# Two transformer layers on one core: where the mixer's fillers stop, and how the compressed queries leave PSUM

## The chip, the cores and the metric

The kernel runs on one core of a Trainium2 chip. All times are device microseconds (us) of one execution. Three timed runs of the kernel before gave 1578.85 us as their median (1576.09 to 1584.00). The execution that was profiled took 1582.09 us; its span, from the first to the last instruction, is 1580.3 us.

Engines are named as in the profile: PE is the matrix engine (PEld its weight loads), DVE the vector engine, ACT the scalar engine, POOL and SP two more whose queues mostly issue DMAs here.

## The reference

Two layers of a diffusion trunk over 512 latent and 128 context tokens, width 1024, all in fp32. One layer is

```
h   = rms_norm(x) * (1 + scale) + shift        # modulation = silu(c) @ w_ada + b_ada
p   = h @ w_in                                 # one projection, split into three head groups
A   = windowed attention, 8 heads, sink         # queries q, keys k, values v
B   = real part of a 2-D Fourier transform      # 256 columns f
C   = latent attention (MLA), 4 heads:
        cq, ckv = rms_norm(compressed q), rms_norm(compressed kv)
        q = cq @ w_uq  (64 plain + 32 rotary columns a head);  k, v = ckv @ w_ukv
x   = x + gate * (concat(A, B, C) @ w_o)
x   = x + gate * mlp(rms_norm(x) * (1 + scale) + shift)   # gated, with a width-3 convolution
```

## The kernel before, in words

**Three passes for each product.** Every fp32 matrix product is three fp32r matmuls: each operand is split into a high part (a rounding copy on ACT) and a low part (source minus high part, on DVE). `hilo` issues that pair: one ACT copy at L125, one DVE subtraction at L144. For weights the same split writes `wh` (ACT) and `wl` (DVE, L188).

**The order of the work.** Each layer has a mixer (attention groups A, B and C; in the span about 80 to 320 us for layer 0 and 870 to 1070 us for layer 1), then the output projection and the MLP, which are dense matmuls. In the mixer a pipeline runs ten units of group A and then five of group C. Each is a chain of scores (PE), maximum (DVE), exponential (ACT), normalisation, transposes (PE, L1051 for A and L1126 for C; copied out as `PT`) and products with the values (PE, L983). While a unit waits for its softmax, other PE work is put in by a generator, `filler()`: the query projections, `fourier`, the compressed projections `cqA`, `cqB` and `ckv`, `rest`, the first part of the output projection (`po0` to `po3`, `part1`), `kv` and `k1` (`mla_kv`) and, in layer 0 only, the modulation chunks 4 to 9 (`ada_pe`). The string `CFG[l]["order"]` gives their sequence.

How much filler goes into a place is decided by `pulls(gen, us)` (L262): it adds up the costs that the generator yields until they reach `us`. A yield of `0` lets the pull go on; a yield of `1e9` ends it. Two places (`pre_c0`, `pre_h2`) pull in a loop with `next(fa)` and ignore the costs. The instructions are then scheduled for each engine by priority, so the final order on an engine is read from the built program.

**What the change touches.**
- `ada_pe` (L307 on): a modulation chunk is 8 matmuls with `wa` tiles loaded by SP (L301, 256 KB each), L320, in four column groups that run side by side, an ACT copy `adasb`, then four transposes (L330).
- `fourier` (L893 on): two products into PSUM, their splits `Z`, then a product with `Z` (`mm<-Z,dftc`).
- `rest` (L795 on): sums of squares by tiny matmuls (L801 to L803), two square roots on ACT (L806, L807), reciprocal and a diagonal on DVE, a spread over PE (L383), the normalised compressed kv (`CL`, `CX`), then three groups `m` of compressed queries, 12 matmuls each (`mm<-cqh,wh` and so on). Group 2 is the rotary part: copied out as `qr`, rotated by four DVE instructions (L639 to L642), split from SBUF. Groups 0 and 1 are the plain part of two heads each.

**Buffers.** `MM()` hands out accumulators for large products from a pool of two; `PS()` small PSUM tiles `s` from a pool of four. `CQ[h]` is the split query of head h. A `part1` accumulator is released by `resid` (L537 on DVE, three instructions for 640 columns).

Of the kernel before, what the change touches and what calls it, by code (L numbers as in the profile page):

```python
# [21 lines left out]
HF = 320  # L22
# [56 lines left out]
def hybrid_step(ctx: ExitStack, tc: tile.TileContext, I, O):  # L79
# [10 lines left out]
    def S(name, dt=F32, w=NT):  # L90
        return sp.tile([128, w], dt, tag="S", name=name)
# [26 lines left out]
    def halves(ap):  # L118
        return ap.rearrange("p (a b) -> p a b", a=2)
# [4 lines left out]
    def acopy(out, in_):  # L124
        return nc.scalar.activation(out, in_, AF.Copy)  # L125
# [10 lines left out]
    def pin(i, on=True):  # L136

        if on:
            tc.keep_in_program_order(i)
        return i  # L140

    def hilo(hi, lo, src, fix=False):
        pin(acopy(hi, src), fix)
        nc.vector.tensor_sub(lo, src, f32(hi))  # L144
# [55 lines left out]
    for l in range(L):  # L200
# [6 lines left out]
        for n in CFG[l]["order"].split():  # L207
# [6 lines left out]
            elif n[:2] == "po":  # L214
                i = int(n[2])
# [88 lines left out]
    def ada_pe(l, chunks, ahead=4):  # L304
        todo = [(n, k) for n in chunks for k in range(8)]
        got = {}

        def load(m):
            while todo and len(got) < m:
                e = todo.pop(0)  # L310
                got[e] = ada_load(l, *e)

        load(ahead)
        yield 0.0
        for n in chunks:
            ps = PS()
            for k in range(8):
                j = k % 4
                t = got.pop((n, k))
                pin(nc.tensor.matmul(ps[32 * j:32 * j + 32, :], lhsT=sT[:, k, :], rhs=t, start=(k < 4), stop=(k >= 4)), l == 0 and n < 4)  # L320
                load(ahead)
                if k % 2:
                    yield 0.45
            lead = l == 0 and n < 4
            sb = S("adasb", w=512)
            pin(acopy(sb, ps), lead)
            yield 0.0
            pt = PS()
            for a in range(4):
                pin(nc.tensor.transpose(pt[:, a * 128:(a + 1) * 128], sb[:, a * 128:(a + 1) * 128], ident), lead)  # L330
            pv = pt.rearrange("p (a j v) -> p a v j", a=4, j=4, v=32)[:, :, 0:2, :]
            parts = ((8 + 2 * n, 0, 2), (2 * n, 2, 2)) if lead else ((4 * n, 0, 4),)
            for i, a, w in parts:
                pin(nc.vector.reduce_sum(out=mod[l][:, i:i + w], in_=pv[:, a:a + w], axis=AX.X), lead)
            for i, a, w in parts:
                m = mod[l][:, i:i + w]
                pin(nc.vector.tensor_add(m, m, P(l, "bada")[:, i:i + w].unsqueeze(2).to_broadcast([128, w, 2])), lead)
                if lead:
                    mod_fin(l, i // 8, (i % 8, w))
            if not lead:  # L340
                mod_fin(l, n // 2, (4 * (n % 2), 4))
            yield -1.0
# [332 lines left out]
    def mixer(l, norm, begun, xsrc):  # L675
# [63 lines left out]
        m = MM()  # L739
# [8 lines left out]
        for t in range(5):  # L748
# [4 lines left out]
            f = S("F", F32R, 512)  # L753
# [12 lines left out]
        CQ, CK, CKX, CV = {}, {}, {}, {}  # L766
# [29 lines left out]
        def rest():  # L796
            ckv = st["ckv"]
            ps = PS()
            for b in range(5):
                sl = slice(QCOL[b], QCOL[b] + 128)  # L800
                nc.tensor.matmul(ps[:, 2 * b:2 * b + 2], lhsT=sq["k"][:, sl], rhs=ones[:, 0:2], start=True, stop=True)  # L801
                nc.tensor.matmul(ps[:, 10 + 2 * b:12 + 2 * b], lhsT=sq["A"][:, sl], rhs=ones[:, 0:2], start=True, stop=False)
                nc.tensor.matmul(ps[:, 10 + 2 * b:12 + 2 * b], lhsT=sq["B"][:64, sl], rhs=ones[:64, 0:2], start=False, stop=True)  # L803
            yield 6.0
            rc = SM("rcC", 20, 1)
            nc.scalar.activation(rc[:, :10], ps[:, :10], AF.Sqrt, bias=eps[:, 0:1], scale=1.0 / 128)  # L806
            nc.scalar.activation(rc[:, 10:], ps[:, 10:20], AF.Sqrt, bias=eps[:, 0:1], scale=1.0 / 192)  # L807
            nc.vector.reciprocal(rc, rc)
            st["rq"], st["nrq"] = SM("rq", 10, 1), SM("nrq", 10, 1)
            nc.vector.tensor_scalar_mul(st["rq"], rc[:, 10:], SC_C)  # L810
            nc.vector.tensor_scalar_mul(st["nrq"], rc[:, 10:], -SC_C)
            rf = MM().rearrange("p a b -> p (a b)")
            for b in range(5):
                spread(rf[:, 128 * b:128 * b + 128], rc[:, 2 * b:2 * b + 1])
            yield 2.2
            for c0, c1, r0 in ((0, NL, 0), (CX, NT, NL)):
                nc.vector.scalar_tensor_tensor(out=ckv[:, c0:c1], in0=ckv[:, c0:c1], scalar=P(l, "gckv"), in1=rf[:, r0:r0 + c1 - c0], op0=ALU.mult, op1=ALU.mult)
            nc.gpsimd.dma_start(out=O["sckv"][l], in_=ckv[:, CX:])
            CL = (S("CL", F32R, 512), S("CL", F32R, 512))
            hilo(CL[0], CL[1], ckv[:, :NL])  # L820
            cx = S("CX", F32R, 512)
            CXh, CXl = cx[:, 0:256], cx[:, 256:512]
            hilo(CXh[:, 128:], CXl[:, 128:], ckv[:, CX:])
            t = S("cc", w=NC)
            gated(nc.gpsimd.dma_start(out=t, in_=I["cckv"][l]))
            hilo(CXh[:, :128], CXl[:, :128], t)
            cq = [st["A"], st["B"]]
            wq = W.get(u["uq"])
            for h in range(4):
                CQ[h] = (S("CQ", F32R), S("CQ", F32R))  # L830
            for m in (2, 0, 1):
                ps = MM()
                for hf in range(2):
                    sl = slice(hf * HF, (hf + 1) * HF)
                    for i, (hi, lo, rows) in enumerate(cq):
                        mm3(ps[:, hf, :HF], [w[:rows, i, m * 128:(m + 1) * 128] for w in wq], [hi[:rows, sl], lo[:rows, sl]], i == 0, i == 1)
                    yield 0.82
                if m == 2:
                    f = S("qr")
                    acopy(halves(f), ps[:, :, :HF])  # L840
                    rope(f, 0, 128, "ropeC", swC)
                    for h in range(4):
                        hilo(CQ[h][0][64:96], CQ[h][1][64:96], f[32 * h:32 * h + 32])
                else:
                    for i in range(2):
                        hi, lo = CQ[2 * m + i]
                        hilo(halves(hi[0:64]), halves(lo[0:64]), ps[64 * i:64 * i + 64, :, :HF])
                yield 0.0
            st["kv"] = lambda: mla_kv(CL, CXh, CXl)

# [48 lines left out]
        def fourier(tabs, tx, tch):  # L899
# [12 lines left out]
            for m in range(2):  # L912
                ps = pz[m]
# [3 lines left out]
                    hilo(Z[q][0][:, :258], Z[q][1][:, :258], ps[:, q, :258])  # L917
                    hilo(Z[q][0][:, 258:], Z[q][1][:, 258:], px[:, m * 256 + q * 128:m * 256 + (q + 1) * 128])
                pz[m] = Z
            yield 0  # L920
            for m in range(2):
                Z = pz[m]
                ps = MM()
# [299 lines left out]
        for c in range(8):  # L1223
            ps = Acc()
# [8 lines left out]
    if True:  # L1233
# [22 lines left out]
        for l in range(L):  # L1256
# [81 lines left out]
            for kind, a in u["plan"]:  # L1338
                if kind == "up":
                    for q, cb in (("a", cb_a(a)), ("g", cb_g(a))):  # L1340
                        ps = Acc()
# [12 lines left out]
                if not last:  # L1354
                    for c in range(8):
                        ps = Acc()
# [3 lines left out]
                else:  # L1360
# [7 lines left out]
                    ps = Acc()  # L1368
# [144 lines left out]
```

## Time and profile before

| | |
|---|---|
| median of 3 runs | 1578.85 us (1576.09 to 1584.00) |
| profiled execution | 1582.09 us |
| its span | 1580.3 us |
| PE busy | 1525.2 us, 97% |
| DVE busy | 1116.7 us, 71% |
| ACT busy | 712.3 us, 45% |
| granted PE clock, mean | 0.984 |

PE is nearly always busy, so what can be saved is the time in which it stands still or runs at the lower clock. Both lie almost wholly in the two mixers. A PE row's `[idle before <-releaser]` tells for how long the engine stood still before that row and which instruction ended the wait. Matmul durations overlap, so the cost of one is read from the distance between two starts.

### The profile page before, as it was taken

The page shows a single profiled execution, that of the slowest core. Times are in us where ns is not written, and L with a number is a line of the kernel's source. Part 1 is how long each engine was busy: PE and PEld are TensorE (multiplying, and loading weights), DVE is VectorE, ACT ScalarE, POOL GpSimd, SP SyncE. Part 2 cuts the span into 40 slices and gives each one's busy share as a digit, 9 for nine tenths or more (in the row PEclk, how much of TensorE's full clock was granted, in tenths as well). Part 3 has the DMA queues.
Part 4 walks back from the last instruction along what each step waited for, and adds up shares of the span by engine and source line. Part 5 has one row for each costly group of instructions (what it writes and reads, how often), then busy time and mean ns, then how long its engine had stood idle before and what let it go on. Part 6 is the DMA issues. An engine that isn't in the chain of part 4 may idle for free. (4 is left out here: it accounts for less than half of the span.)

```text
span 1580.3 us, 25827 instructions
## 1 busy us (share of the span) xinstructions
PE 1525.2 (97%) x10082; PEld 1426.3 (90%) x10082; DVE 1116.7 (71%) x2257; ACT 712.3 (45%) x1403; POOL 103.7 (7%) x225
## 2 busy tenths in 40 slices
PE   9999989899999999999999999989999999999997
PEld 7977775599999999999999887869999999999997
DVE  5765674477897888889778777867885466466366
ACT  4555664564432432441445666646433243244142
POOL 1200111100000000001011000120000000000000
PEclk9999999899999999999999999999999999999998
DMA  9542239113334335235244202331332222221211
GB/s 363 166 145 74 73 98 312 56 54 120 116 124 169 120 104 196 104 104 193 81 142 133 72 25 86 114 142 54 120 99 75 81 74 61 94 77 52 100 54 67
DMA packets 61800, 177.59 MB, mean 112 GB/s; under 512 B 7360, under 2 KB 9856, under 8 KB 61680
## 3 DMA queue, kind: packets, MB, share of 16 engines
q1 hardware_dynamic: 44112, 116.41, 22.1%
q0 software_dynamic: 17568, 59.55, 11.2%
q8 instruction: 79, 1.29, 0.3%
q14 instruction: 41, 0.34, 0.1%
HBM read 165.02 MB, written 10.91 MB: 111 GB/s over the span
## 5 line engine op out<-in xcount | busy, mean ns | idle before, releaser
L278 PE MATMUL mm<-hh,wh 128*128 128x320 f32 x1632 | 377.5, 312 | 12.3 <-ACT u L125 9.1
L278 PE MATMUL mm<-hl,wh 128*128 128x320 f32 x1632 | 377.2, 310 | 0.7 <-DVE hl L486 0.4
L278 PE MATMUL mm<-hh,wl 128*128 128x320 f32 x1632 | 376.9, 310 | 0.0
L125 ACT ACTIVATE wh<-wr 128x1024 fp32r<-128x1024 f32 (+2 forms) x189 | 185.9, 984 | 343.1 <-PE mm L278 263.9
L278 PEld LDWEIGHTS mm<-hh,wh 128*128 128x128 f32 x1632 | 273.8, 188 | 20.6 <-ACT u L125 11.0
L278 PEld LDWEIGHTS mm<-hl,wh 128*128 128x128 f32 x1632 | 275.6, 188 | 4.0 <-issue 2.1
L278 PEld LDWEIGHTS mm<-hh,wl 128*128 128x128 f32 x1632 | 274.5, 188 | 3.3 <-issue 3.3
L188 DVE TENSOR_TENSOR wl<-wr,wh 128x1024 fp32r<-128x1024 f32 (+2 forms) x187 | 210.9, 1128 | 48.2 <-ACT wh L125 47.3
L1292 DVE SCALAR_TENSOR_TENSOR y<-u,pk,y 128x642 f32<-128x642 f32 x176 | 156.2, 887 | 67.9 <-ACT y L1289 64.2
L278 PE MATMUL mm<-th,wh 128*128 128x320 f32 x656 | 152.4, 310 | 0.0
L278 PE MATMUL mm<-th,wl 128*128 128x320 f32 x656 | 152.2, 309 | 0.0
L278 PE MATMUL mm<-tl,wh 128*128 128x320 f32 x656 | 152.0, 309 | 0.0
L537 DVE SCALAR_TENSOR_TENSOR x<-mm,mod,x 128x192 f32<-128x192 f32 (+2 forms) x222 | 84.9, 435 | 70.6 <-PE mm L278 70.6
L364 DVE CUSTOM_DVE_ANT_0 junk<-wa,sbc 128x1024 bf16<-128x1024 f32 x112 | 132.1, 1223 | 1.8 <-DMA wa<-in_wat 1.8
L1289 ACT ACTIVATE y<-u,bb,pk 128x513 f32<-128x513 f32 (+1 forms) x176 | 105.9, 650 | 60.8 <-DVE bb L1286 60.8
L278 PEld LDWEIGHTS mm<-th,wh 128*128 128x128 f32 x656 | 110.3, 188 | 0.7 <-ACT th L125 0.4
L278 PEld LDWEIGHTS mm<-th,wl 128*128 128x128 f32 x656 | 110.4, 188 | 0.0
L278 PEld LDWEIGHTS mm<-tl,wh 128*128 128x128 f32 x656 | 110.4, 188 | 0.0
L1282 DVE TENSOR_TENSOR u<-mm,r 128x512 f32<-128x512 f32 (+1 forms) x176 | 79.6, 486 | 42.2 <-PE mm L278 40.1
L125 ACT ACTIVATE u<-mm 128x2 f32<-128x2 f32 x176 | 20.8, 170 | 112.5 <-DVE u L1282 107.5
L1306 ACT ACTIVATE y<-y 128x642 f32<-128x642 f32 x44 | 32.6, 741 | 73.7 <-DVE y L1292 73.7
L361 POOL DMA_DIRECT2D wa<-in_wat x56 | 29.5, 528 | 524.2 <-DVE mod L364 517.8
(311 smaller groups left out, 2195.6 us busy)
## 6 DMA issues: line engine op xcount, KB each, us to landing
wr<-in_wug SPq DMA_DIRECT2D x88, 512.0 KB, 3.5
wa<-in_wat POOLq DMA_DIRECT2D x56, 512.0 KB, 3.8
wa<-in_wa SPq DMA_DIRECT2D x80, 256.0 KB, 5.7
wr<-in_wdn SPq DMA_DIRECT2D x48, 384.0 KB, 3.1
wr<-in_wi SPq DMA_DIRECT2D x16, 512.0 KB, 3.7
wr<-in_wo SPq DMA_DIRECT2D x14, 512.0 KB, 3.7
xpart<-xp POOLq DMA_DIRECT2D x16, 320.0 KB, 3.7
x<-xpart POOLq DMA_DIRECT2D x16, 320.0 KB, 6.1
```

The source lines that it names most:

```text
L125: return nc.scalar.activation(out, in_, AF.Copy)
L188: pin(self.eng.tensor_sub(lo, r, f32(hi)), fix)
L278: pin(nc.tensor.matmul(ps.h[hf][:, :c1 - c0], lhsT=w[wi][:, off[k] if isinstance(off, dict) else k + off, :], rhs=hs[hi][k][:, c0:c1], sta ...
L361: nc.gpsimd.dma_start(out=t, in_=I["wat"][i0 + i])
L364: nc.vector.tensor_tensor_reduce(out=junk, in0=t, in1=sb[v], scale=1.0, scalar=0.0, op0=ALU.mult, op1=ALU.add, accum_out=mod[l][:, n, v:v ...
L537: nc.vector.scalar_tensor_tensor(out=xc[:, c0:c1], in0=ps.h[hf][:, o:o + c1 - c0], scalar=mod[l][:, gidx * 8 + c, v:v + 1], in1=xc[:, c0:c ...
L1282: nc.vector.tensor_mul(halves(uu[:, p:p + n]), ps.t[:, :, o:o + n // 2], halves(nrm.r[:, c0:c1]))
L1289: nc.scalar.activation(y[:, c0:c1], uu[:, c0 + 1:c1 + 1], AF.Identity, bias=bb[:, v:v + 1], scale=cv[:, t, 1:2])
L1292: nc.vector.scalar_tensor_tensor(out=yy, in0=uu[:, q:q + TW], scalar=cv[:, t, q:q + 1], in1=yy, op0=ALU.mult, op1=ALU.add)
L1306: nc.scalar.activation(y, y, AF.Silu)
```

## The change

```diff
@@ ada_pe
             lead = l == 0 and n < 4
             sb = S("adasb", w=512)
             pin(acopy(sb, ps), lead)
-            yield 0.0
+            yield 0.0 if lead else 1e9
             pt = PS()
@@ rest
-            for m in (2, 0, 1):
+            for m in (0, 1, 2):
                 ps = MM()
...
                 else:
+                    f = S("qn")
+                    acopy(halves(f), ps[:, :, :HF])
                     for i in range(2):
-                        hi, lo = CQ[2 * m + i]
-                        hilo(halves(hi[0:64]), halves(lo[0:64]), ps[64 * i:64 * i + 64, :, :HF])
+                        hilo(CQ[2 * m + i][0][0:64], CQ[2 * m + i][1][0:64], f[64 * i:64 * i + 64])
                 yield 0.0
@@ fourier
                 pz[m] = Z
-            yield 0
+            yield 1e9
             for m in range(2):
```

A filler now ends its pull after the copy of a modulation chunk (not for the four leading chunks) and after the splits `Z` of the Fourier product. Groups 0 and 1 of the compressed queries come before the rotary group, and each leaves its accumulator by one ACT copy into an SBUF tile `qn`, from which both splits are then taken (before: two ACT copies and two DVE subtractions straight from PSUM). The number of instructions on PE and DVE is unchanged; ACT has four copies more and two `ACT_TABLE_LOAD` more. Lines below L845 move down by one.

On DVE in layer 0, where the compressed queries are split; before (`CQ<-mm` reads the accumulators `mm_2109` and `mm_2126`, `CQ<-qr` the rotated tile):

```order
L642 TENSOR_TENSOR qr_2094<-qr_2094,ropes_2096 128x512
L144 TENSOR_TENSOR CQ_2058<-mm_2109,CQ_2057 64x640
L144 TENSOR_TENSOR CQ_2058<-qr_2094,CQ_2057 32x640
L188 TENSOR_TENSOR wl_2382<-wr_2183,wh_2381 128x1024
L144 TENSOR_TENSOR CQ_2060<-qr_2094,CQ_2059 32x640
L144 TENSOR_TENSOR CQ_2060<-mm_2109,CQ_2059 64x640
L144 TENSOR_TENSOR CQ_2062<-qr_2094,CQ_2061 32x640
L144 TENSOR_TENSOR CQ_2062<-mm_2126,CQ_2061 64x640
L144 TENSOR_TENSOR CQ_2064<-qr_2094,CQ_2063 32x640
```

And after, the end of the same work on DVE, with the `L537` instructions that release the first `po1` accumulator (`mm_2182`):

```order
L144 TENSOR_TENSOR CQ_2080<-qn_2146,CQ_2079 64x640
L639 STREAM_SHUFFLE ropes_2167<-qr_2165 128x512
L640 TENSOR_TENSOR ropes_2167<-ropes_2167,ropeC_1414 128x512
L641 TENSOR_TENSOR qr_2165<-qr_2165,ropeC_1413 128x512
L144 TENSOR_TENSOR ml_1823<-s_2233,mh_1822 128x128
L642 TENSOR_TENSOR qr_2165<-qr_2165,ropes_2167 128x512
L1037 TENSOR_TENSOR den_2113<-den_2113,d_2115 128x4
L537 SCALAR_TENSOR_TENSOR xp_2180<-mm_2182,mod0_86,xp_2180 128x320
L537 SCALAR_TENSOR_TENSOR xp_2180<-mm_2182,mod0_86,xp_2180 128x192
L144 TENSOR_TENSOR CQ_2074<-qr_2165,CQ_2073 32x640
L144 TENSOR_TENSOR CQ_2076<-qr_2165,CQ_2075 32x640
L144 TENSOR_TENSOR CQ_2078<-qr_2165,CQ_2077 32x640
```

No subtraction reads an accumulator of the compressed queries any more; the rotation and the splits `CQ<-qr` have moved to the end, and a fourth split and the third `L537` follow the rows shown.

On PE at the end of layer 0's fillers, before (`L320` are matmuls of the last modulation chunk, `L330` its transposes, `CKb,CQ` and `CKX,CQ` scores of group C):

```order
L320 MATMUL s<-wa,sT 32x512
L983 MATMUL s<-PT,CV 64x256 x3
L320 MATMUL s<-wa,sT 32x512
L286 MATMUL mm<-CKb,CQ 128x320 x5
L330 MATMUL s<-ident,adasb 128x128 x4
L983 MATMUL s<-PT,CV 64x256 x2
L286 MATMUL mm<-CKb,CQ 128x320
L1126 MATMUL s<-ident,P 128x128 x12
L286 MATMUL mm<-CKb,CQ 128x320 x17
L983 MATMUL s<-PT,CV 64x256 x2
L1126 MATMUL s<-ident,P 128x128 x4
```

And after (the first `L330` is chunk 8's, the second chunk 9's):

```order
L330 MATMUL s<-ident,adasb 128x128 x4
L1127 MATMUL s<-ident,P 128x128 x4
L320 MATMUL s<-wa,sT 32x512 x2
L984 MATMUL s<-PT,CV 64x256 x4
L320 MATMUL s<-wa,sT 32x512 x2
L286 MATMUL s<-CKX,CQ 128x256 x6
L320 MATMUL s<-wa,sT 32x512 x2
L1127 MATMUL s<-ident,P 128x128 x4
L320 MATMUL s<-wa,sT 32x512 x2
L1127 MATMUL s<-ident,P 128x128 x4
L286 MATMUL s<-CKX,CQ 128x256 x3
L330 MATMUL s<-ident,adasb 128x128 x4
```

Chunk 9 has moved into the last softmax units: of the 37 scores `CKb,CQ` that followed it before, 12 still do, and the first scores `CKX,CQ` stand among its matmuls.

On ACT in layer 1, the two square roots of `rest`, before:

```order
L806 ACT_TABLE_LOAD
L806 ACTIVATE rcC<-s,eps 128x10
L807 ACTIVATE rcC<-s,eps 128x10
L1033 ACT_TABLE_LOAD
L1033 ACTIVATE d<-d 128x4
L125 ACTIVATE PT<-s 128x512
```

And after:

```order
L806 ACT_TABLE_LOAD
L806 ACTIVATE rcC<-s,eps 128x10
L1033 ACT_TABLE_LOAD
L1033 ACTIVATE P,den<-s,negm 128x128 x4
L125 ACTIVATE mh<-s 128x128
L807 ACT_TABLE_LOAD
L807 ACTIVATE rcC<-s,eps 128x10
L125 ACTIVATE mh<-s 128x128
```

Four exponentials and two table loads now stand between the two roots. On SP the only difference is in layer 0: where the last 12 loads of `wa` (for chunks 8 and 9) stood in a row ahead of all loads of `wug`, the first `wug` load now stands ahead of the last 12, and the second ahead of the last 10. On POOL loads and stores of `xp` change places in layer 0.

## Rows read from the trace of the kernel before

**Rows 1.** Page, busy time by engine: us, share of the span, instructions.

```profile
PE 1525.2 (97%) x10082; PEld 1426.3 (90%) x10082; DVE 1116.7 (71%) x2257; ACT 712.3 (45%) x1403; POOL 103.7 (7%) x225
```

**Rows 2.** Windows: length, busy time of each engine, granted PE clock, DMA share, GB/s.

```profile
80.00:320.00 240.00, 224.11 (x1364) 169.15 (x1363) 139.82 (x375) 136.42 (x312) 23.50 (x60) 0.95 0.37 124
870.00:1070.00 200.00, 189.19 (x1243) 161.22 (x1243) 148.84 (x380) 121.34 (x282) 23.35 (x60) 0.97 0.26 86
241.00:249.00 8.00, 6.47 (x32) 1.61 (x31) 1.82 (x7) 1.75 (x5) 0.54 (x1) 1.00 1.04 395
278.00:304.00 26.00, 20.44 (x124) 13.62 (x122) 12.15 (x34) 13.59 (x34) 4.90 (x20) 0.92 0.12 44
```

**Rows 3.** Timeline of PE, compressed queries of layer 0: start, duration, instruction, idle before.

```profile
188.25 0.39 PE L286 MATMUL mm<-cqh,wh 128*128 128x320 f32 x1
...
196.46 0.51 PE L1008 MATMUL s<-KH,Q 128*128 128x512 f32 x1
...
202.25 0.87 PE L278 MATMUL mm<-mh,wh 128*128 128x320 f32 x2 [3.67 <-DVE CQ L144]
...
207.72 0.39 PE L278 MATMUL mm<-ml,wh 128*128 128x320 f32 x1
...
210.74 0.45 PE L278 MATMUL mm<-ml,wh 128*128 128x320 f32 x2
211.03 0.46 PE L278 MATMUL mm<-mh,wl 128*128 128x320 f32 x2
```

**Rows 4.** Timeline of DVE at the same place.

```profile
199.18 1.22 DVE L188 TENSOR_TENSOR wl<-wr,wh 128x1024 fp32r<-128x1024 f32 x1
...
201.28 0.82 DVE L144 TENSOR_TENSOR CQ<-mm,CQ 64x640 fp32r<-64x640 f32 x1
...
204.68 0.69 DVE L1011 CUSTOM_DVE_ANT_0 P<-s,mask 128x512 f32<-128x512 f32 x1
...
210.52 1.13 DVE L537 SCALAR_TENSOR_TENSOR xp<-mm,mod,xp 128x320 f32<-128x320 f32 x3
```

**Rows 5.** Timeline of ACT at the same place.

```profile
190.88 0.70 ACT L125 ACTIVATE qr<-mm 128x640 f32<-128x640 f32 x1
```

**Rows 6.** Timeline of PE, Fourier product of layer 0.

```profile
103.29 1.86 PE L286 MATMUL mm<-Z,dftc 128*128 128x386 f32 x7 [1.12 <-DVE Z L144]
```

**Rows 7.** Timeline of PE, modulation chunks 6 and 7.

```profile
241.12 1.07 PE L320 MATMUL s<-wa,sT 128*32 128x512 f32 x8
242.98 0.66 PE L330 MATMUL s<-ident,adasb 128*128 128x128 f32 x4 [0.80 <-ACT adasb L125]
243.56 4.50 PE L320 MATMUL s<-wa,sT 128*32 128x512 f32 x16
248.80 0.66 PE L330 MATMUL s<-ident,adasb 128*128 128x128 f32 x4 [0.74 <-ACT adasb L125]
```

**Rows 8.** Timeline of SP: DMA issues, start of the first, time from first to last.

```profile
245.95 14.52 SPq L301 DMA_DIRECT2D wa<-in_wa  x12
263.73 59.71 SPq L168 DMA_DIRECT2D wr<-in_wug  x3
```

**Rows 9.** Timeline of PE, the softmax units at the end of layer 0's mixer.

```profile
304.16 0.90 PE L278 MATMUL mm<-mh,wh 128*128 128x320 f32 x2 [2.05 <-ACT P L1105]
```

**Rows 10.** Timeline of PE, `rest` of layer 1 behind the tiny sums.

```profile
953.55 0.58 PE L1008 MATMUL s<-KH,Q 128*128 128x256 f32 x1
...
959.76 0.83 PE L383 MATMUL mm<-diag,ones 128*128 128x128 f32 x6
...
963.61 0.42 PE L286 MATMUL mm<-cqh,wh 128*128 128x320 f32 x1
```

**Rows 11.** Timeline of ACT, the two roots and the table load behind them in layer 0.

```profile
182.31 0.26 ACT L807 ACTIVATE rcC<-s,eps 128x10 f32<-128x10 f32 x1
182.59 1.28 ACT L1032 ACT_TABLE_LOAD   x1
183.89 0.37 ACT L1032 ACTIVATE P<-s,negm 128x128 f32<-128x128 f32 x1
```

## The prediction

> **What bounds the kernel now.** I read the busy times first: PE works 1525.2 of 1580.3 us [rows 1], so only its idle time and its time at the lower clock can be won. Then the windows, to see where that lies: in the two mixers PE stands idle for 15.9 us (240.00 less 224.11) and 10.8 us (200.00 less 189.19), at a mean granted clock of 0.95 and 0.97 [rows 2]. Then the timeline of PE in them, with the releaser of each wait. Three kinds are touched here:
>
> - PE waits 3.67 us for a DVE subtraction `CQ`, because the first output-projection matmuls need an accumulator that still holds compressed queries; it then runs at the low level of its clock: the 20 matmuls from 202.25 to 207.72 take 5.47 us, where a pair takes 0.29 a little later, so 2.9 for 20; 2.5 us lost [rows 3].
> - At modulation chunks 6 and 7 PE waits 0.80 and 0.74 us for the copy `adasb`, and the eight matmuls of chunk 7 stretch over 4.50 us [rows 7] while the DMA engines are full (share 1.04, 395 GB/s) [rows 2].
> - In the last softmax units of layer 0, with no filler left, PE is idle for 5.6 of 26.0 us at clock 0.92 [rows 2], and once more 2.05 us before 304.16 [rows 9], of which 1.9 lie in those 5.6.
>
> DVE and ACT are half idle over each mixer [rows 2], but not at these places: there their order decides.
>
> **The change, part by part.** The sum is made against the profiled execution (1582.09 us, of which 1580.3 are span), 3.2 us above the median of the three runs; I carry the difference over to the median.
>
> *Compressed queries, layer 0.* Removed: the 3.67 us and the 2.5 behind it, 6.2 together. Both accumulators of groups 0 and 1 now leave by one ACT copy each; `qr`, a copy of the same form, takes 0.70 [rows 5], and PE has another group (2.7 us, a third of the 8.2 from 188.25 to 196.46 [rows 3]) to run meanwhile. But DVE's work is the same, and part of it now stands ahead of `L537`, which frees the first `po1` accumulator for the products `CL`. I add both paths from the first compressed-query matmul. PE: 8.2 for the queries; eight 512-column scores took 2.12 (196.46 to 198.58, where the wait begins), four of them remain on this path, 1.1; twice 24 output-projection matmuls at 0.147, 7.0; eight 384-column scores at three quarters of the longer ones, 1.6; six small ones at 0.17 (four in 0.66 [rows 7]), 1.0: PE asks for the accumulator at 18.9. DVE: it starts at 2.7 + 0.7 + 0.7 = 4.1; eight `CQ` at 0.82, 6.6; four maxima at 0.69, 2.8; one weight split 1.22; four rotary steps, taken as 0.69 as well, 2.8; three `L537`, 1.13 [rows 4]; some small ones, 1.2 by my estimate: 19.8. So 0.9 us of wait comes back if DVE never waits itself. At most all of the old 3.67 with its 2.5 does. I take 1.5, near the lower end, since the sum's terms are measured and only ACT's interleaving can add. **−4.7 us** (−6.2 to 0). The added ACT copies, two a layer, cost nothing as long as ACT, busy for 136 of 240 us [rows 2], gets to them inside the next group; if not, each adds its 0.7 to the wait just named.
>
> *Modulation chunks.* Chunk 6's transposes now stand 28 matmuls behind its last one: 0.80 goes. Chunk 7 starts later by these matmuls, and its loads have that time to land: of its 4.50 us two groups of four, 1.06 each (241.12 to 242.18, where the wait of 0.80 begins), are work, so 2.4 go. Against it: matmuls of a chunk that are pulled apart run in more groups. By the order chunks 6 and 7 have three groups each where there were two, chunks 8 and 9 together seven where there were eight: +1.06. Chunk 7's transposes still follow directly on its last group, so 0.74 stays; chunk 8's now do too, +0.74. Sum −0.80 − 2.4 + 1.06 + 0.74 = **−1.4 us** (−3.2 if the new groups hide in other waits, +1.8 if the loads still set the pace).
>
> *The last softmax units.* Chunks 8 and 9 used to end ahead of 37 scores `CKb,CQ`; now 12 remain behind them, and chunk 9's four groups (4.2 us) lie in the stretch where PE waited for `P`. The stake is 5.6 us of idle time, 1.6 for the clock (8% of 20.4) and the 0.2 left of the last wait: 7.4. The chunks also leave a place where they hid some wait before, so not all 4.2 count. I take **−3.5 us**, half the stake (−7.4 to 0).
>
> *Fourier.* The order of PE is the same word for word up to 113 us, so the 1.12 us in front of the product with `Z` [rows 6] stays: **0**. What moves behind it is in the other terms.
>
> *Layer 1.* Before, 6.2 us pass from the last tiny sum to the spread `L383`, 953.55 to 959.76 [rows 10]; 24 matmuls lie in them, at about half clock, so some 3.1 are lost. Now those 24 stand ahead of the sums, and on ACT four exponentials and two table loads lie between the roots. Chain: root 0.26, load 1.28, four exponentials 1.5, a copy 0.3, load 1.28, root 0.26 [rows 11]: 4.9; reciprocal, scalings and diagonals on DVE, at most 0.3 each by the 512-column price of rows 4, 1.5. PE has eight 512-column scores and eight products with values to cover them, 3.0. Lost: 6.4 − 3.0 = 3.4 instead of 3.1. Queued behind the second root on ACT is the split `CL`, needed only later. There is no stall of layer 0's size to remove at the accumulators here, but DVE's order puts `L537` behind `CQ<-qr` as well; +0.4. Sum **+0.7 us** (−3.1 to +4.4, the whole lengthening of ACT's chain).
>
> Here a rule speaks against the change. In layer 0 a root ends at 182.57, the load runs from 182.59 to 183.87 and the next exponential starts at 183.89 [rows 11]: a switch costs 1.3 us. The Trainium skill (ScalarE: Activation LUTs, section "What ACT_TABLE_LOAD costs") adds a drain of about 1.38 us to each load, some 2.66 for a switch; by it the two extra loads would cost 2.8 us more. The trace shows no room for that drain.
>
> *Queues.* SP's first `wug` loads move ahead of `wa` loads, each waiting for a weight split on DVE. I cost this at nothing while that split ends before chunk 8 begins; what it costs otherwise is the second rival. POOL's exchanged loads and stores of `xp` are hidden by the units between them; a late one would delay `L537` alone.
>
> Sum: −4.7 − 1.4 − 3.5 + 0 + 0.7 = −8.9 us, that is 1573.2 for the profiled execution and **1570** against the median.
>
> **The rivals.**
>
> *The wait is given back.* DVE is the bound between `rest` and `CL`: `L537` comes as late as the old split did, with the same low clock. The first term is then 0, layer 1 pays 2 us for the same reason, the other two terms stay at −4.9: −2.9, **1576**. For it: DVE's path (19.8) is already the longer one. Against it: by 0.9 us only. Chance 0.15.
>
> *The fillers do not do what they say.* Two of four modulation chunks keep their transposes right behind their copy, and the Fourier product keeps its place. If the chunks' terms come to nothing, −4.7 + 0.7 = −4.0 remains, **1575**. Chance 0.10.
>
> *Slower: the modulation loads arrive late.* The second `wug` load waits on SP for a split on DVE that stands behind six `L537` just ahead of chunk 8, and ten `wa` loads are queued behind it. Before, the last 12 `wa` issues went out from 245.95 over 14.52 us, to 260.5, and the first `wug` only at 263.73 [rows 8]. If that buffer comes free no earlier, twelve loads at their old pace end at 278.2, 17.8 us later than before. Chunk 9 then had some 8 us in hand (its last matmuls were issued near 274, a load lands in under 6), so PE would wait about 10 us, fall to the low clock for another 2.5 as in rows 3, and gain nothing at the last units: −4.7 − 1.4 + 0.7 + 12.5 = +7 and, with the modulation chunks' own gain gone as well, +8.5: **1587**. It decides from the point where the split ends more than some 2 us after chunk 8's first matmul. Against it: the order places the split ahead of that matmul's neighbours on DVE. Chance 0.13.
>
> *Table switches cost twice the row.* By the rule above +2.8, **1573**; rows 11 speak against it. Chance 0.04.
>
> *Everything goes.* Halfway to the lower ends of all terms (−6.2 − 3.2 − 7.4 − 3.1 = −19.9): −14.5, **1564**. Chance 0.10.
>
> **How the numbers follow.** The forecast has 0.48; its own range is 1566 to 1575. The range of 1562 to 1583 leaves out part of the slower rival and a little below. About 0.5% (7.9 us) is what a measurement of this kernel can tell from no change. Faster than 1571: some 0.35 of the forecast's 0.48 and the 0.10 of everything: 0.45. Slower than 1586.7: most of the slower rival and a little for what I did not think of: 0.14. The rest, 0.41, lies between.
>
> **What would show it.** In the changed profile the `mm<-mh` matmuls behind the compressed queries start without a wait on `CQ`, and the products `CL` of layer 0 carry a wait of 1 to 2 us that DVE's `L537` ends. Chunk 6's transposes carry none, those of chunks 7 and 8 about 0.75 each. Between chunk 9 and the next output-projection matmuls PE is idle for about 3 us instead of 7. In layer 1 ACT shows three table loads close together, and `L383` starts some 6 us after the sums. The prediction is wrong if PE waits at chunks 8 and 9 for `wa`, if the wait at `CL` reaches the old 3.67, or if layer 1's mixer grows by more than 4 us.

## The result: slower, and the profile after

The changed kernel takes 1598.74 us (median of four runs, 1598.44 to 1601.09) against 1580.69 (1576.09 to 1584.00): a ratio of 1.0118, 95% interval 1.0099 to 1.0137. The forecast was 1570 and faster; even the range, up to 1583, ends below it. The profiled run took 1601.09 us, 1599.3 of them span, at a mean granted clock of 0.979 (before 0.984).

The page of after, busy time by engine, beside [rows 1]: the work is the same in number, PE's busy time is 7.4 us longer (behind a wait the matmuls of these runs often stand at the low level of the clock: a pair `CL,wh` takes 1.19 us behind the wait of 3.57 below, at a granted clock of 0.50, and 0.63 in E11 without a wait, at 209.53 and a clock of 1.00) and its idle time 11.6 us longer (1599.3 − 1532.6 against 1580.3 − 1525.2).

```profile
PE 1532.6 (96%) x10082; PEld 1427.5 (89%) x10082; DVE 1116.1 (70%) x2257; ACT 716.9 (45%) x1409; POOL 103.4 (6%) x225
```

The windows of after over the two mixers (columns as in [rows 2]):

```profile
80.00:320.00 240.00, 221.06 (x1361) 166.09 (x1361) 139.00 (x373) 136.87 (x312) 23.42 (x60) 0.96 0.37 125
870.00:1070.00 200.00, 184.02 (x1173) 153.88 (x1171) 140.91 (x363) 118.46 (x272) 20.90 (x55) 0.93 0.25 79
```

Layer 0 gets through as many matmuls as before (1361 against 1364). Layer 1 gets through 1173 in the time in which it did 1243, and its clock falls from 0.97 to 0.93. As every kernel here issues 10082 matmuls, I measure a mixer as the time from one matmul to another by their count: the 589th to the 1801st for layer 0 (94.6 to 312.8 us before), the 5501st to the 6681st for layer 1 (870.7 to 1061.8). After, layer 0 is 0.2 us longer and **layer 1 14.4 us**. In layer 0 that evenness goes with the clock: PE stands idle for 18.9 us between the two matmuls instead of 15.9, at a granted clock of 0.96 instead of 0.95. In layer 1 it stands idle for 18.6 instead of 10.8. Of the other 4.4 us, 1.3 lie ahead of layer 0's mixer and 2.3 behind it, where PE's order is unchanged.

**Layer 0.** The wait of 3.67 us for `CQ` is gone. PE of after, from the first matmul of the compressed queries to the products `CL`:

```profile
189.25 0.40 PE L286 MATMUL mm<-cqh,wh 128*128 128x320 f32 x1
...
200.11 0.65 PE L984 MATMUL s<-PT,V 128*64 128x256 f32 x4 [1.49 <-ACT PT L125]
...
206.07 0.56 PE L278 MATMUL mm<-mh,wh 128*128 128x320 f32 x2 [0.56 <-ACT qr L125]
...
213.91 1.19 PE L286 MATMUL mm<-CL,wh 128*128 128x512 f32 x2 [3.57 <-DVE den L1038]
```

And DVE there:

```profile
201.75 0.82 DVE L144 TENSOR_TENSOR CQ<-qn,CQ 64x640 fp32r<-64x640 f32 x1 [0.26 <-ACT CQ L125]
204.63 0.82 DVE L144 TENSOR_TENSOR CQ<-qn,CQ 64x640 fp32r<-64x640 f32 x1 [2.06 <-ACT CQ L125]
...
209.01 0.87 DVE L537 SCALAR_TENSOR_TENSOR xp<-mm,mod,xp 128x320 f32<-128x320 f32 x2
209.91 3.49 DVE L144 TENSOR_TENSOR CQ<-qr,CQ 32x640 fp32r<-32x640 f32 x4
213.41 0.35 DVE L537 SCALAR_TENSOR_TENSOR xp<-mm,mod,xp 128x128 f32<-128x128 f32 x1
```

The wait has come back at `CL` with nearly its old size. Four rotary splits, 3.49 us in one piece, stand between the second and the third `L537`, and the accumulator is free only behind the third, at 213.76. (The view names the short `den` that runs on DVE beside its end.) The 1221st matmul (207.72 before) is 5.1 us early; the 1335th (225.96 before) is 1.1 us late: all 6.2 us were given back. Not all of that is the queries' doing. Between the same two matmuls the queries alone (E2, below) lose 3.7 us against before, and the chunks alone (E3) 3.1.

PE at chunks 6 to 9 and at the last softmax units, beside [rows 7, 9]:

```profile
258.01 0.66 PE L330 MATMUL s<-ident,adasb 128*128 128x128 f32 x4 [0.72 <-ACT adasb L125]
...
280.33 1.05 PE L320 MATMUL s<-wa,sT 128*32 128x512 f32 x2 [0.52 <-DMA wa<-in_wa]
282.46 1.04 PE L320 MATMUL s<-wa,sT 128*32 128x512 f32 x2 [1.08 <-DMA wa<-in_wa]
284.19 1.00 PE L330 MATMUL s<-ident,adasb 128*128 128x128 f32 x4 [0.69 <-ACT adasb L125]
...
306.88 0.56 PE L278 MATMUL mm<-mh,wh 128*128 128x320 f32 x2 [2.05 <-ACT P L1106]
```

The issues of SP, beside [rows 8]:

```profile
256.16 0.33 SPq L168 DMA_DIRECT2D wr<-in_wug  x1
...
270.86 0.33 SPq L168 DMA_DIRECT2D wr<-in_wug  x1
271.28 11.52 SPq L301 DMA_DIRECT2D wa<-in_wa  x10
```

The last ten `wa` loads go out from 271.28 to 282.80, 22 us later than before, and PE waits 1.6 us for them. The slower rival named this place; the wait is small here.

**Layer 1.** PE of after; before, the longest wait between 955 and 1049 us is 1.34 (at 979.20):

```profile
965.81 0.50 PE L1009 MATMUL s<-KH,Q 128*128 128x512 f32 x1 [0.83 <-ACT rcC L807]
...
992.93 2.83 PE L984 MATMUL s<-PT,V 128*64 128x256 f32 x12 [3.80 <-DVE d L1020]
...
1010.44 0.65 PE L1052 MATMUL s<-ident,P 128*128 128x128 f32 x4 [1.57 <-DVE xp L537]
...
1016.40 1.22 PE L286 MATMUL mm<-CL,wh 128*128 128x512 f32 x2 [2.05 <-ACT P L1106]
...
1053.40 1.70 PE L286 MATMUL mm<-CKb,CQ 96*128 96x320 f32 x5 [2.05 <-ACT P L1106]
```

DVE ahead of the longest: the same block of four splits, and behind it the `negm`, the copy `PT` and the `d` that PE needs.

```profile
988.44 3.51 DVE L144 TENSOR_TENSOR CQ<-qr,CQ 32x640 fp32r<-32x640 f32 x4
991.98 0.16 DVE L1019 SCALAR_TENSOR_TENSOR negm<-mx,nsink 128x4 f32<-128x4 f32 x1
992.09 0.69 DVE L134 COPY PT<-s 128x512 f32<-128x512 f32 x1
```

### The profile page after: what moved, and what is told of

The parts are those of the page before. It is cut to its first block, busy times and chain, and to the rows that moved or that the text cites. A ratio compares the mean times of both kernels' runs of the same rounds, so it can differ in the third digit from the quotient of the medians.

```text
span 1599.3 us, 25852 instructions
## 1 busy us (share of the span) xinstructions
PE 1532.6 (96%) x10082; PEld 1427.5 (89%) x10082; DVE 1116.1 (70%) x2257; ACT 716.9 (45%) x1409; POOL 103.4 (6%) x225
## 5 line engine op out<-in xcount | busy, mean ns | idle before, releaser
L278 PEld LDWEIGHTS mm<-hh,wh 128*128 128x128 f32 x1632 | 275.4, 188 | 21.6 <-ACT u L125 10.7
L537 DVE SCALAR_TENSOR_TENSOR x<-mm,mod,x 128x192 f32<-128x192 f32 (+2 forms) x222 | 84.8, 436 | 70.2 <-PE mm L278 69.7
```

What stands on the lines that cost most here:

```text
L278: pin(nc.tensor.matmul(ps.h[hf][:, :c1 - c0], lhsT=w[wi][:, off[k] if isinstance(off, dict) else k + off, :], rhs=hs[hi][k][:, c0:c1], sta ...
L537: nc.vector.scalar_tensor_tensor(out=xc[:, c0:c1], in0=ps.h[hf][:, o:o + c1 - c0], scalar=mod[l][:, gidx * 8 + c, v:v + 1], in1=xc[:, c0:c ...
```

## The experiments

Times are medians, each against the kernel before measured beside it. The two columns at the right are the change in length of the mixers, from one profile each, and in brackets the change of PE's idle time in them (15.9 and 10.8 us before). The lengths carry 2 to 4 us of spread: in the layer 0 of E1 and E5 and in the layer 1 of E8 PE's order is that of before, and yet they read −2.0, −3.2 and +3.7. The spread is mostly the clock. E5's layer 0 has the waits of before and as much idle time, at a granted clock of 0.96 instead of 0.95. The idle times are steadier: where PE's order is that of before they read −0.1 to 0.0 in layer 0 and +0.7 to +1.3 in layer 1.

| run | us | before | ratio, 95% interval | layer 0 (idle) | layer 1 (idle) |
|---|---|---|---|---|---|
| after | 1598.74 | 1580.69 | 1.0118 (1.0099 to 1.0137) | +0.2 (+3.0) | +14.4 (+7.8) |
| E1 Fourier alone | 1593.12 | 1579.26 | 1.0081 (1.0055 to 1.0106) | −2.0 (0.0) | +10.1 (+6.2) |
| E2 queries alone | 1585.44 | 1579.26 | 1.0035 (1.0016 to 1.0053) | −3.7 (−1.6) | +4.3 (+4.1) |
| E3 chunks alone | 1587.52 | 1579.26 | 1.0047 (1.0029 to 1.0064) | +5.5 (+5.7) | −0.4 (+1.3) |
| E4 queries and chunks | 1590.05 | 1579.26 | 1.0062 (1.0044 to 1.0079) | 0.0 (+2.5) | +5.4 (+4.5) |
| E5 Fourier, rest carried | 1580.49 | 1580.89 | 1.0000 (0.9984 to 1.0016) | −3.2 (−0.1) | +1.4 (+0.7) |
| E6 rotary splits later | 1587.23 | 1580.89 | 1.0044 (1.0023 to 1.0064) | +0.5 (0.0) | +4.4 (+2.2) |
| E7 chunks 4, 5 | 1590.08 | 1580.89 | 1.0067 (1.0043 to 1.0092) | +4.7 (+4.9) | −0.6 (+0.9) |
| E8 chunks 6 to 9 | 1585.81 | 1580.89 | 1.0039 (1.0021 to 1.0058) | +0.5 (+3.6) | +3.7 (+1.2) |
| E9 splits on POOL | 1588.57 | 1579.85 | 1.0064 (1.0047 to 1.0081) | −0.4 (−0.1) | +6.3 (+5.2) |
| E10 chunks 4, 5, carried | 1586.32 | 1579.85 | 1.0050 (1.0028 to 1.0073) | +4.6 (+7.3) | −0.5 (+1.2) |
| E11 copies, old order | 1583.54 | 1579.85 | 1.0026 (1.0013 to 1.0039) | −3.4 (−0.7) | +5.1 (+2.9) |
| E12 queries, layer 0 alone | 1578.57 | 1579.68 | 0.9991 (0.9977 to 1.0006) | −3.8 (−1.6) | −1.0 (+0.7) |
| E13 chunks, loads early | 1585.48 | 1579.68 | 1.0031 (1.0014 to 1.0047) | +0.9 (+5.0) | +1.8 (+0.9) |

**E1 to E4: the parts.** E1 is the kernel before with

```diff
-            yield 0
+            yield 1e9
```

in `fourier`. E2 has the change's edit of `rest`:

```diff
-            for m in (2, 0, 1):
+            for m in (0, 1, 2):
...
+                    f = S("qn")
+                    acopy(halves(f), ps[:, :, :HF])
...
```

E3 has the edit of `ada_pe`, and E4 both of the last:

```diff
-            yield 0.0
+            yield 0.0 if lead else 1e9
```

Expected of E1: 

> The kernel before with one edit: the yield behind the Fourier splits is 1e9. By the order only layer 1's mixer differs from before (218 matmuls moved, none in layer 0). Theory F (ending that pull shifts all later fillers of layer 1 away from the softmax waits that they covered): slower by 9 to 15 us, all of it between 870 and 1090 us; products with the values stand idle once for 3 to 4 us as in the changed kernel. Theory C (the compressed queries cost the time: their splits, the release of the first po1 accumulator and the two table loads): within 4 us of before.

Of E2: 

> The kernel before with the edit in rest alone: order 0, 1, 2 and one copy out of each accumulator. Theory F: in layer 0 the old wait of 3.67 us goes and 3 to 4 us come back at CL, so 0 to -3 us there; layer 1 within 3 us of before; total -4 to +2. Theory C: layer 1 loses 9 to 15 us between the tiny sums and the scores CK,CQ; total +7 to +15.

Of E3: 

> The kernel before with the edit in ada_pe alone; by the order only layer 0's mixer differs. Theory F: within 4 us of before, since the changed kernel's layer 0 came out even with before's while the queries took 5 us out of it until their accumulator wait: -2 to +4. Theory C has the same layer 0 and says nothing else: -2 to +4. If it is above +5, the queries do gain in layer 0 and the chunks give it back.

Of E4: 

> The changed kernel without the Fourier yield (chunks and queries only). Theory F: layer 1 as in e2, layer 0 as in the changed kernel (even with before): total -3 to +3 against before, some 15 us below the changed kernel. Theory C: layer 1 keeps its loss: +8 to +16 against before.

Each part alone is slower. Theory F holds for E1 (+13.9 us), but it had E2, E3 and E4 near the time before, and they are 6.2, 8.3 and 10.8 us slower: Fourier is the largest part and not the only one. E1's 10.1 and E2's 4.3 make the 14.4 of layer 1 in after, and E2's −3.7 and E3's +5.5 come near its layer 0, within the spread. The times do not add up: the three ratios together make 1.63%, after has 1.18%. With the other two parts in place the Fourier yield costs 0.56% (after against E4), alone 0.81%. In E1 PE waits in layer 1 where it hardly did before (1.45 at 1003.17 and 2.05 at 1043.87 are two more):

```profile
976.99 0.53 PE L278 MATMUL mm<-mh,wh 128*128 128x320 f32 x2 [2.92 <-DVE CQ L144]
...
1007.86 0.73 PE L286 MATMUL mm<-CL,wh 128*128 128x512 f32 x2 [2.05 <-ACT P L1105]
```

The reason for the first is on DVE. In E1 four maxima of a softmax unit and a `PT` copy stand ahead of the rotation and the splits:

```profile
966.35 0.68 DVE L1011 CUSTOM_DVE_ANT_0 P<-s,mask 128x512 f32<-128x512 f32 x1
...
969.95 0.72 DVE L639 STREAM_SHUFFLE ropes<-qr 128x512 f32<-128x512 f32 x1
...
976.02 0.83 DVE L144 TENSOR_TENSOR CQ<-mm,CQ 64x640 fp32r<-64x640 f32 x1
```

Before, the maxima came behind them, and PE waited 0.42 at the same matmuls (the last row is PE's):

```profile
967.02 0.72 DVE L639 STREAM_SHUFFLE ropes<-qr 128x512 f32<-128x512 f32 x1
...
972.63 0.82 DVE L144 TENSOR_TENSOR CQ<-mm,CQ 64x640 fp32r<-64x640 f32 x1
...
976.01 0.69 DVE L1011 CUSTOM_DVE_ANT_0 P<-s,mask 128x512 f32<-128x512 f32 x1
...
973.60 0.52 PE L278 MATMUL mm<-mh,wh 128*128 128x320 f32 x2 [0.42 <-DVE CQ L144]
```

PE asks for the accumulator at 974.07 in E1 and at 973.18 before (the start of its matmul less the wait). The rotation begins 4.1 us ahead of that in E1 and 6.2 before, so it is 2.0 us later; from its first step to the split that PE waits for it is 6.1 us and 5.6. The two together make the 2.5 us by which the wait grew. After has the waits of 1.57, 2.05 and 2.05 in common with E1, but in place of the 2.92 it has the 3.80 shown above: the parts meet in the same stretch and the waits change their places. The two table loads between the roots are in E1 too and not in E2, so they belong to Fourier.

In E2's layer 1 the block of splits tears `L537` apart, here between its first step and its second, and PE waits 4.37 us at `CL` (983.54):

```profile
977.68 0.54 DVE L537 SCALAR_TENSOR_TENSOR xp<-mm,mod,xp 128x320 f32<-128x320 f32 x1
978.36 3.49 DVE L144 TENSOR_TENSOR CQ<-qr,CQ 32x640 fp32r<-32x640 f32 x4
...
983.05 0.34 DVE L537 SCALAR_TENSOR_TENSOR xp<-mm,mod,xp 128x128 f32<-128x128 f32 x1
```

**E5: is it the cut at the Fourier copy, or the shift behind it?** A pull is the filler time that the builder asks for between two units. By its amounts the cut ends a pull of 6.3 us in layer 1 at 4.5, and all later fillers move back; in layer 0 it falls on a pull with nothing left. E5 keeps the cut and adds what is left to the next pull:

```diff
-        done = 0.0
+        done, us, owed[0] = 0.0, us + owed[0], 0.0
...
+            if c == 2e9:
+                owed[0] = us - done
+                break
...
-            yield 0
+            yield 2e9
```

> As e1, but what the cut pull did not take (1.9 us of filler) is added to the next pull. By the order PE then stands as before from shortly behind the Fourier product on (29 matmuls moved, none after the first quarter of layer 1's mixer). Theory S (the loss of e1 is the shift: each later filler of layer 1 comes one step late for the softmax it covered): layer 1's mixer within 1.5 us of before, total -2 to +3. Rival (the cut itself costs, at the place where the pull ends): layer 1 keeps 6 to 10 us.

Measured: no difference, 1.0000 (0.9984 to 1.0016). By the order 29 matmuls stand elsewhere than before, and at the place of the 2.92 PE waits 0.66:

```profile
972.00 0.52 PE L283 MATMUL mm<-mh,wh 128*128 128x320 f32 x2 [0.66 <-DVE CQ L144]
```

So the cut by itself costs nothing that shows here (the interval allows 2.5 us), and the shift of the later fillers makes E1's loss.

**E6: are the rotary splits at fault by their place?** Rotation and splits move into `mla_kv`, behind the first key step:

```diff
-                    rope(f, 0, 128, "ropeC", swC)
-                    for h in range(4):
-                        hilo(CQ[h][0][64:96], CQ[h][1][64:96], f[32 * h:32 * h + 32])
...
+            rope(qr, 0, 128, "ropeC", swC)
+            for h in range(4):
+                hilo(CQ[h][0][64:96], CQ[h][1][64:96], qr[32 * h:32 * h + 32])
```

> As e2 (queries only), but the rotation of qr and its four splits CQ<-qr are issued behind the first key product of mla_kv, so that on DVE they stand behind both releases of the output-projection accumulators. Theory L (e2's wait of 2.5 and 4.4 us at CL is L537 standing behind those splits): these waits fall under 1 us, layer 0 is 5 to 8 us faster than before and layer 1 0 to 4 us, total -4 to -11. Rival (DVE has too much work there in any order): the wait moves to CX or to the scores CK,CQ, total within 3 us of e2.

Measured: 1.0044, no better than E2. The waits at `CL` are gone. In layer 1 one of 2.27 us for a high part `CQ` (ACT) stands at the scores `CK,CQ` instead (999.77), as the rival said, and in layer 0 two stand where the block is now:

```profile
221.59 1.12 PE L984 MATMUL s<-PT,V 128*64 128x256 f32 x4 [2.21 <-DVE PT L134]
...
233.34 0.66 PE L1052 MATMUL s<-ident,P 128*128 128x128 f32 x4 [2.01 <-DVE xp L537]
```

So Theory L fell: moving the block does not win the time back. The rival came true; that DVE has too much work there in any order is its reading, and this run does not prove it.

**E7, E8, E10: which chunks.** E7 cuts at chunks 4 and 5 only, E8 at 6 to 9 only; E10 is E7 with the carry of E5.

```diff
-            yield 0.0
+            yield 0.0 if lead or n >= 6 else 1e9
```

E7: 

> Of the edit in ada_pe only chunks 4 and 5 end a pull; 6 to 9 yield 0 as before. Theory S (the chunks' loss of 5 us is filler lost at the cut pulls, 4.9 us at chunk 4, so that later softmax steps stand uncovered): +3 to +6 us, with the wait for PT of about 3 us near 226 us as in e3. Rival D (the chunks' own price: more groups of matmuls, transposes behind their copies, late loads at chunks 8 and 9): within 1.5 us of before.

E8: 

> Only chunks 6 to 9 end a pull; 4 and 5 as before, so that up to 230 us PE's order is that of before. Theory S: within 2 us of before, no wait near 226 us. Rival D: +3 to +6 us, with waits on wa loads and on adasb copies after 240 us as in e3.

E10: 

> As e7, but what a cut pull left is added to the next one. Theory S (the loss is the shift of later fillers): layer 0's mixer within 2 us of before, no wait of 3 us for PT near 226 us and none of 4 us for wa loads near 279 us. Rival (the cut's own place, or the transposes' later start): +3 to +6 remain.

Both halves cost. E7 lengthens layer 0 by 4.7 us with 4.9 us more idle time, in three waits above all. The first is 0.4 longer than before; near the second there was one of 1.08 (225.96); the third is new:

```profile
201.82 0.87 PE L278 MATMUL mm<-mh,wh 128*128 128x320 f32 x2 [4.06 <-DVE CQ L144]
...
228.18 0.65 PE L983 MATMUL s<-PT,V 128*64 128x256 f32 x4 [3.32 <-DVE PT L134]
...
279.42 1.92 PE L320 MATMUL s<-wa,sT 128*32 128x512 f32 x2 [3.90 <-DMA wa<-in_wa]
```

Chunks 6 to 9, for which I had forecast a gain, cost as well. E8's length of layer 0 reads only +0.5 because its clock was 0.97 instead of 0.95; PE is idle there for 3.6 us more, and the time is 1.0039. Its waits of more than 0.2 us from 240 us to the last softmax unit add up to 11.3 us instead of 7.2, 1.5 of them for `wa` (none before) and 2.8 for the copies `adasb` (1.5 before): the rival of E8, not Theory S. The halves do not add up to E3 (5.7 us of idle time). E10 keeps +4.6, with waits of 5.72 at the first place (203.43), 3.31 (229.93) and 3.91 (280.05): here the carry does not help, and the explanation of E5 does not hold for the chunks.

**E9: does DVE's load decide?** E9 is E2 with three of each layer's eight splits on POOL.

```diff
+                        (nc.gpsimd if h == 2 else nc.vector).tensor_sub(CQ[h][1][64:96], f[32 * h:32 * h + 32], f32(CQ[h][0][64:96]))
...
+                        acopy(hi[0:64], f[64 * i:64 * i + 64])
+                        (nc.vector if i else nc.gpsimd).tensor_sub(lo[0:64], f[64 * i:64 * i + 64], f32(hi[0:64]))
```

> As e2 (queries only), but three of the eight subtractions CQ (0.82 us each on DVE) run on POOL, so DVE has 2.5 us less ahead of the L537 that frees the accumulator for CL. Theory B (DVE is the bound between rest and CL; only less work there helps): the waits at CL fall from 2.5 and 4.4 us to 0 to 1 and 2 to 3, none comes back at CX or CK,CQ, layer 0 -5 to -7 and layer 1 -1 to +3 against before, total -6 to 0. Rival (the position of L537 alone matters, as e6 showed none of it): as e2 or e6, +3 to +7.

Measured: 1.0064. In layer 0 the wait at `CL` falls to 0.72 (213.24), but one of 4.27 stands just ahead of it, for a DVE split `ml` at the scores (211.55). In layer 1 PE's wait at `CL` grows to 6.83 us (989.72). DVE and POOL there:

```profile
982.25 1.74 DVE L844 TENSOR_TENSOR CQ<-qr,CQ 32x640 fp32r<-32x640 f32 x2
984.02 1.64 DVE L1044 TENSOR_SCALAR P<-P,den 128x512 f32<-128x512 f32 x1
...
988.44 1.13 DVE L537 SCALAR_TENSOR_TENSOR xp<-mm,mod,xp 128x320 f32<-128x320 f32 x3 [0.77 <-DMA xp<-xd]
```

```profile
983.69 1.69 POOL L844 TENSOR_TENSOR CQ<-qr,CQ 32x640 fp32r<-32x640 f32 x1 [6.66 <-ACT CQ L125]
985.33 0.56 POOL L947 DMA_DIRECT2D xp<-xd  x1
```

POOL issues the load of `xp` behind its split and `L537` waits for that load; a DVE step beside the split took 1.64 us. In each layer two DVE steps were stretched in this way (last section), by 1.3 us together in layer 0 and about 2.5 in layer 1. So DVE was not freed of the 2.5 us that the run was to take from it; Theory B's gains did not come, and the run does not tell whether DVE's load is the bound.

**E11, E12: copies and order apart.** E11 has the copies with the groups in the old order, E12 the edit of E2 in layer 0 alone:

```diff
-            for m in (2, 0, 1):
+            for m in (0, 1, 2) if l == 0 else (2, 0, 1):
```

E11: 

> As e2, but the groups of the compressed queries stay in the old order 2, 0, 1: the rotary group first, then the copies qn. Theory B (DVE's sum of work decides, not which split is last): the old wait of 3.67 us at the first po1 matmul goes, 2 to 4 us come back at CL in both layers as in e2, total 0 to +5. Rival (the rotary group's place at the end is what costs in e2): no wait over 1 us at CL, layer 0 -4 to -7, layer 1 -2 to +1, total -8 to -2.

E12: 

> The edit in rest as in e2, in layer 0 only; layer 1 stands on every engine as before. Theory A (the parts add up by layer: e2's layer 0 gained 3.7 us and its layer 1 lost 4.3): layer 0 -3 to -4.5, layer 1 within 1.5 of before, total -1 to -5, the only version so far below before. Rival (e2's gain in layer 0 was the state of the clock in one execution, and the timed median counts): total 0 to +4.

E11 has no wait over 1 us at `CL`; it waits 2.71 us for the copy `qn` in layer 0 (199.31) and 3.34 for a maximum in layer 1 (972.23), where it loses as much as E2. Neither expectation holds: the wait at `CL` goes, as the rival said, but layer 1 does not gain. By one profile each, layer 1 pays for the copies with either order. E12 is the best version found, at 0.9991 not to be told from before. Its mixer of layer 0 has three waits from 196 to 232 us, of 2.53, 0.81 and 0.38, where before there were four, of 3.67, 1.08, 0.30 and 0.24:

```profile
210.38 1.08 PE L286 MATMUL mm<-CL,wh 128*128 128x512 f32 x2 [2.53 <-DVE xp L537]
```

**E13: how much of the chunks' loss is the load queue?** E3 with the `wa` loads of the last four chunks issued up to eight ahead:

```diff
-CFG[0]["ahead"] = (8, 4)
+CFG[0]["ahead"] = (8, 8)
```

> As e3 (chunks only), with eight wa loads issued ahead for chunks 6 to 9 instead of four, so that chunk 8's last two loads stand ahead of the second wug load on SP. Theory Q (part of the chunks' loss is that queue): the two waits of PE for wa (0.5 and 1.1 us near 284 us) go, the last softmax units of layer 0 end 2 to 4 us earlier than in e3. Rival (the loads are not on the path, PE waits for P there anyway): within 1 us of e3 at the end of layer 0's mixer.

PE's waits for `wa` fall from 1.60 to 0.11 us. Layer 0's lengthening falls from 5.5 to 0.9, but its idle time only from 21.6 to 20.9 us: two other waits have come, 2.11 at 174.91 and 1.91 for the copy `adasb` at 262.56. Behind the second `wug` load, issued at 277.91, only six now stand:

```profile
278.33 3.79 SPq L301 DMA_DIRECT2D wa<-in_wa  x6
```

The intervals of E3 and E13 overlap, and a wait of 3.33 for `PT` (232.29) stays. So the queue makes the waits for `wa`, as the first half of Theory Q says; that it makes a part of the loss in time is not shown.

## Why the prediction was wrong

**The step that failed is the term "Fourier", 0.** I had followed PE's order to the product with `Z` in layer 0, found it the same, and wrote that what moves behind is in the other terms. It was in none: in layer 1 the cut pushes 1.9 us of fillers (by the builder's amounts), and all behind them, one place on. Alone it makes the kernel slower by 0.8% (E1, 10.1 us in layer 1's mixer), and with the fillers put back by nothing (E5). Its wait in layer 0, taken to stay at 1.12, did (1.14).

It is not the only step that failed. The forecast was 9 us faster and the result is 18 us slower; of these 27 us the Fourier yield makes 9 (after against E4) to 13 (E1). Without it the kernel is still slower (E4, 1.0062), because the chunks and the queries, from which I expected the gain, cost time as well.

**Compressed queries, layer 0, −4.7.** Mechanism and place were right: the wait at `CQ` went and one ended by `L537` came at `CL`. The size was off. It is 2.53 in E2 and E12 and 3.57 in after, against 1.5 taken. I let DVE start at 4.1 us and never wait; it stood idle for 2.06, 0.67 and 0.26 us for ACT, the condition that I had named. Of the gain of 4.7, 1.6 us of idle time are shown: by so much PE's idle time in layer 0 falls with the queries alone, in E2 and again in E12. The rest of their −3.7 and −3.8 is no more than layer 0 shows in E1 and E5 with PE's order unchanged (−2.0, −3.2). E12's time gains 1.1 us with an interval that holds zero.

**Layer 1, +0.7.** The range went to +4.4; the queries alone measured +4.3 (E2, 4.1 of it idle time). The 0.4 for `L537` behind the splits was the term that was too small: in E2 it is a wait of 4.37. The chain of roots and table loads, 3.4 of the sum, came as written (four table loads, 956.08 to 973.03), but it let PE stand idle for 0.83 us only:

```profile
960.38 0.27 ACT L806 ACTIVATE rcC<-s,eps 128x10 f32<-128x10 f32 x1 [3.02 <-PE s L803]
960.66 1.28 ACT L1033 ACT_TABLE_LOAD   x1
961.95 0.37 ACT L1033 ACTIVATE P<-s,negm 128x128 f32<-128x128 f32 x1
```

The exponential starts 0.01 us behind the load's end (960.66 + 1.28). The drain that the Trainium skill (ScalarE: Activation LUTs, section "What ACT_TABLE_LOAD costs") adds is not there; that rival falls.

**Modulation chunks and the last softmax units, −1.4 and −3.5.** Together −4.9; measured alone +5.5 in layer 0 (5.7 of it idle time) and a ratio of 1.0047 (E3). Chunk 6's wait went as forecast, chunk 7 paid 0.72, and the wait of 2.04 for `P` behind the last chunk (282.69 before) went too. But I priced chunks 6 to 9 by the waits that I saw before, and others came in their place: alone they make 3.6 us more idle time (E8). And I never priced chunks 4 and 5, which the same edit cuts (E7, 4.9 us). At the last units PE still waits 2.05 us. Why the cut costs at the chunks, where the carry does not help (E10), and what the shares of the three waits in E7 are, stays open.

**Two readings.** DVE is not half idle over each mixer: in layer 1's it is busy for 148.84 of 200 us [rows 2], so work put in its way there finds less room. And of PE's 55.1 us of idle time before, 26.7 lie in the two mixers, about half and not almost all.

**The rivals.** "The wait is given back" is right as a mechanism: in E2, from the start of layer 0's mixer on, 6.7 us are won up to the 1221st matmul and 3.7 of them lost again by the 1335th. Its 2 us for layer 1 are too few. "Modulation loads arrive late" is there with 1.6 us instead of 10. The slower outcome itself came by a path that none of them had. Of my signs of being wrong two came, the wait for `wa` at chunk 8 and a layer 1 more than 4 us longer; the wait at `CL`, 3.57, stopped just short of the third.

## What to carry to other kernels

In a kernel whose fillers are handed out by time, ending one pull early is an edit of everything that is handed out after it; compare the order of all engines to the end of the stage, and price each place where two engines' orders changed against each other. A wait on an accumulator moves to the next accumulator if the same in-order engine empties both: look for blocks of work put in the middle of the group of instructions that releases one (here 3.5 us of splits between the second and third of three `L537`). Read the idle time of a stretch beside its length: the length carries what the clock did in that one execution. Try an edit stage by stage; one that helps in one layer can cost in the other.

## What the runs showed of the hardware

**The same kernel's time goes with the granted clock.** Of 75 executions of the kernel before, timed beside the experiments, the fastest took 1572.74 us at a mean granted clock of 0.991 and the slowest 1584.54 at 0.981. The profiled one (0.984) lies in the slower half. What the engine's waits were in the timed ones is not on record.

**A DVE step slows beside POOL.** In E9 four DVE steps that began while a split ran on POOL took longer than elsewhere. A `P<-P,den` of 128x512 took 1.64 us, from 984.02 to 985.66, while a POOL split ran from 983.69 to 985.38; in the kernel before the longest of 40 such steps in both mixers took 0.49. Two splits `CQ` took 1.37 and 1.55 (192.76, 207.89) instead of 0.82, and a split `CX` took 1.63, while in layer 0 of the same run it took 0.29:

```profile
966.81 1.56 POOL L851 TENSOR_TENSOR CQ<-qn,CQ 64x640 fp32r<-64x640 f32 x1 [3.61 <-ACT CQ L125]
...
966.89 1.63 DVE L144 TENSOR_TENSOR CX<-cc,CX 128x128 fp32r<-128x128 f32 x1 [2.96 <-ACT CX L125]
```

All four ended 0.16 to 0.69 us behind POOL's split. A split `ml`, which reads one of its inputs from PSUM, took its 0.29 beside POOL (192.00). The Trainium skill (SBUF — State Buffer, section "SBUF: two separate sides") has the two engines share a port pair that one holds for its whole instruction, on DVE's side for a step in a two-port mode or with two inputs in SBUF; these rows agree, though none shows whether `P<-P,den` ran in such a mode. Spans on POOL are rough. The six splits on POOL took 1.52 to 1.69 us; on DVE they take 0.82.
